# Down projection of a two-layer decoder trunk: the weight sums for the third half-size product, from GpSimd to VectorE

## The chip, the cores and the metric

The kernel runs on one core of one Trainium2 chip. The metric is the device time of one execution in microseconds (us). The kernel before takes 1276.46 us, the median of 3 runs between 1275.83 and 1279.62 us.

## The reference

The reference is a decoder trunk of two layers on 512 tokens of width 1024, in fp32. Layer 0 has sparse attention and a memory cross-attention, layer 1 dilated attention and a memory cross-attention, and each layer ends in the same squared-ReLU MLP. Only the MLP is touched here:

```python
def squared_relu_mlp(h, w_up, w_down):
    return jnp.square(jax.nn.relu(h @ w_up)) @ w_down

x = x + squared_relu_mlp(rmsnorm(x, mlp_norm[layer]), w_up[layer], w_down[layer])
```

`w_up` is 1024 x 4096, `w_down` 4096 x 1024.

## The kernel before

**Precision.** Every fp32 operand of a matrix product is split in a high part (fp32r) and a low part (the rest). `wsplit` does this for weights: ScalarE copies the high part (L237), VectorE subtracts it from the source to get the low part (L239). `split` does it for activations (L282 on ScalarE, L285 on VectorE). `mm3` then issues three matmuls: high by high (L244), and twice high by low (L247), first the one with the low part of the weights, then the one with the low part of the activations.

**The MLP.** The hidden width of 4096 is done in four quarters (the loop over `q` in `mlp`), in each of the two layers, so there are eight quarters in all. A quarter makes eight tiles of 128 hidden columns (the up projection), squares them, and then multiplies them with a 1024 x 1024 block of `w_down`. That product is a Strassen-Winograd scheme: seven products of half size in place of eight. Its operands are sums of blocks. The activation sums are made in `combos` (L1145 and the splits that follow), the weight sums in `addto` (L1131), a loop that adds a loaded block to two tiles of 128 x 512 in place.

**Order of the products in a quarter**, each 24 matmuls for each of two halves `h` of the inner dimension, 48 in all where both halves count:

1. `w11`: block B11 as loaded, into banks of the pool `acc`. Its split is that of a loaded tile `st`. Beside it GpSimd adds B11 to the tiles `U`.
2. `w3`: the pieces `T` (two tiles `x` for each half), which hold B22 - B12 as loaded and summed earlier, into banks of the pool `ps`. After the split, `addto(t, t, b11[h])` adds B11 to the same tiles.
3. `w2`: these new `T`, the third half-size product, into banks of the pool `pt`, against the activation sums `s2` (tiles `act`). After the split, `addto` adds B21 to `T`.
4. `w4`: `T` once more, into the banks `ps` again, which `into` (L1333) has emptied in between.
5. `w1`: the pieces `U`, into new banks `pt`, against `s1`; then `w22` and `w21`, which are blocks as loaded.

So a piece of `T` goes round: split by ScalarE and VectorE, sum, split, sum, split. A sum must wait until both parts of the split before it have been read, and the next split waits for the sum. An instruction of one engine waits for another engine's by a semaphore, and each engine works its own list strictly in order. That order comes from a scheduler that plays the program through; it is fixed when the kernel is built.

**Buffers.** The pool `x` has 8 tiles, `w` 4 split weight tiles, `st` 3 loaded tiles. A tile `st` that holds B11 is free for the next load once the sum that reads it is done.

**First quarter of a layer.** Its VectorE list is further behind TensorE than that of the three others, and the running totals `G` are started by two copies on ScalarE (L1345), where the other quarters add on VectorE (L1337).

Of the kernel before, what the change touches and what calls it, by code (L numbers as in the profile page):

```python
# [12 lines left out]
ALU = mybir.AluOpType  # L13
# [154 lines left out]
class K:  # L168
# [956 lines left out]
            nc.vector.tensor_tensor(out=self.x[m], in0=ps, in1=xo, op=ALU.add)  # L1125


    def addto(self, out, a, b):

        for i, (o, x) in enumerate(zip(out, a)):  # L1130
            self.nc.gpsimd.tensor_tensor(out=o, in0=x, in1=b[:, i * 512 : (i + 1) * 512], op=ALU.add)  # L1131

    def wpieces(self, t):

# [21 lines left out]
    def mlp(self, l):  # L1156


        nc, ins = self.nc, self.ins
        H = S // 2  # L1160
        x = self.x
# [74 lines left out]
        for q in range(4):  # L1236
            a, A12, A4 = [None] * 8, [], []
            B = [ins["w_db"][l, q, i] for i in range(4)]
            U, T = [], []
            for n in range(8):  # L1240
# [32 lines left out]
                if n in (5, 6):  # L1273

                    t = [self.t("x", [P, 512]) for _ in range(2)]
# [16 lines left out]
            b11 = []  # L1292
# [11 lines left out]
            def w3(h):  # L1304

                t = T[2 * h : 2 * h + 2]
                w = self.wpieces(t)
                self.addto(t, t, b11[h])
                return w

            def w2(h):
# [31 lines left out]
            for u in range(2):  # L1343
                if q == 0:
                    nc.scalar.activation(G[u], X[u], AF.Copy)  # L1345
                else:
                    add(G[u], X[u])
            product(Z, blk(0, H), w3)
            into(Z, 1, 1, True)
            Y = two(self.pT)  # L1350
# [463 lines left out]
```

## Time and profile before

| | |
|---|---|
| median of 3 runs | 1276.46 us |
| the profiled execution's own time | 1277.1 us |
| its span, first to last instruction | 1275.3 us |
| mean granted TensorE clock | 0.997 |
| TensorE matmuls busy | 1240.4 us, 97% |
| VectorE busy | 990.8 us, 78% |
| ScalarE busy | 763.3 us, 60% |
| GpSimd busy | 469.4 us, 37% |
| sums on GpSimd (L1131) whose tiles are `x` on both sides | 64, mean 1681 ns |

The row of a timeline holds the start in us, the duration in us (of the whole run of equal instructions, where `xN` is over 1), the engine, the line, the operation with output and inputs, and in brackets how long the engine had stood idle and what released it. In the rows of windows each engine has its busy time and the number of instructions, and PEclk is the granted TensorE clock. A matmul of 512 columns is shown with 0.39 us, but the next one begins about 0.227 us later, so TensorE is filled when starts follow at that distance.

### The profile page before, as it was taken

What the parts mean: (1) busy time and instruction counts of PE and PEld (TensorE: products, weight loads), DVE (VectorE), ACT (ScalarE), POOL (GpSimd) and SP (SyncE); (2) the same over time, 40 slices, a digit from 0 to 9 for tenths busy, and PEclk for the clock granted to TensorE, in tenths of its full rate; (3) what the DMA queues carried; (4) which work ended last, traced back from release to release, by engine and by line L of the source; (5) the groups of instructions that cost most, each with busy time, mean ns of one, the idle gap of its engine ahead of it and who ended that gap; (6) DMA issues with size and microseconds to landing.
All of it is one profiled execution on the core that took longest, in us unless ns stands there. A gap on an engine that the chain in (4) does not pass through costs nothing.

```text
span 1275.3 us, 18580 instructions
## 1 busy us (share of the span) xinstructions
PE 1240.4 (97%) x6445; PEld 1013.5 (79%) x6445; DVE 990.8 (78%) x1745; ACT 763.3 (60%) x1763; POOL 469.4 (37%) x497
## 2 busy tenths in 40 slices
PE   9998999999999999999999999999999999999998
PEld 8776777677787887888888899888688788888886
DVE  6868878864669678687799968887679868779687
ACT  6666767773466464554656567887776455464462
POOL 0666464533165142260342612222435226034241
PEclk9999999999999999999999999999999999999999
DMA  8312311023432525325235332113241532624423
GB/s 312 112 58 69 100 34 59 10 75 106 151 99 77 175 79 171 125 83 185 97 98 179 104 116 64 62 35 96 69 155 67 178 124 79 187 94 139 141 83 116
DMA packets 52718, 139.11 MB, mean 109 GB/s; under 512 B 5680, under 2 KB 14896, under 8 KB 52624
## 3 DMA queue, kind: packets, MB, share of 16 engines
q1 hardware_dynamic: 51568, 135.50, 33.4%
q0 software_dynamic: 480, 1.38, 0.3%
q8 instruction: 51, 0.84, 0.3%
q10 hardware_dynamic: 576, 1.05, 0.2%
q14 instruction: 43, 0.35, 0.1%
HBM read 132.66 MB, written 5.24 MB: 108 GB/s over the span
## 4 chain that ended last, share of the span: by engine, by line
PE 74%; DVE 17%; ACT 4%; issue 2%; DMA 1%; POOL 1%; SPq 0%; POOLq 0%; DVEq 0%; ACTq 0%
PE s_ps L247 23%; PE s_acc L247 12%; PE s_ps L244 11%; DVE s_w L239 6%; PE s_acc L244 6%; PE s_pt L247 5%; PE s_pt L244 3%; DVE s_p L1145 2%; PE s_po L1080 2%; DVE s_qk L285 1%; PE s_acc L845 1%; ACT s_w L237 1%; PE s_pt L1067 1%; PE s_ps L1031 1%; DVE s_pt L1333 1%
## 5 line engine op out<-in xcount | busy, mean ns | idle before, releaser
L247 PE MATMUL s_ps<-s_act,s_w 128*128 128x512 f32 x1184 | 366.0, 390 | 0.0
L239 DVE TENSOR_TENSOR s_w<-s_st,s_w 128x1024 fp32r<-128x1024 f32 (+4 forms) x161 | 191.1, 1189 | 133.5 <-ACT s_w L237 133.2
L247 PEld LDWEIGHTS s_ps<-s_act,s_w 128*128 128x128 f32 x1184 | 221.8, 188 | 45.7 <-DVE s_act L285 0.4
L237 ACT ACTIVATE s_w<-s_st 128x1024 fp32r<-128x1024 f32 (+4 forms) x182 | 165.7, 918 | 131.0 <-PE s_pt L247 35.6
L244 PE MATMUL s_ps<-s_act,s_w 128*128 128x512 f32 x592 | 231.6, 393 | 3.1 <-DVE s_x L817 1.7
L247 PE MATMUL s_acc<-s_w,s_act 128*128 128x512 f32 (+2 forms) x608 | 169.7, 360 | 2.0 <-DVE s_w L239 1.5
L1131 POOL TENSOR_TENSOR s_x<-s_x,s_st 128x512 f32<-128x512 f32 x64 | 106.0, 1681 | 90.8 <-DVE s_w L239 90.8
L244 PEld LDWEIGHTS s_ps<-s_act,s_w 128*128 128x128 f32 x592 | 110.9, 188 | 28.4 <-ACT s_act L282 3.2
L247 PEld LDWEIGHTS s_acc<-s_w,s_act 128*128 128x128 f32 x608 | 108.9, 190 | 13.1 <-DVE s_w L239 1.6
L244 PE MATMUL s_acc<-s_w,s_act 128*128 128x512 f32 (+2 forms) x304 | 111.0, 370 | 1.9 <-ACT s_w L237 1.9
L1131 POOL TENSOR_TENSOR s_x<-s_qki,s_st 128x512 f32<-128x512 f32 x16 | 26.5, 1654 | 214.9 <-DMA s_st<-in_w_db_dram 195.3
L676 POOL TENSOR_SCALAR s_p<-s_p,s_cr 128x256 f32<-128x256 f32 (+3 forms) x128 | 68.0, 545 | 71.6 <-DVE s_cr L1043 33.4
L239 DVE TENSOR_TENSOR s_w<-s_x,s_w 128x512 fp32r<-128x512 f32 x96 | 88.7, 965 | 5.6 <-ACT s_w L237 5.6
L247 PE MATMUL s_pt<-s_w,s_act 128*128 128x512 f32 x288 | 90.0, 399 | 2.6 <-DVE s_w L239 2.6
L285 DVE TENSOR_TENSOR s_qk<-s_p,s_qk 128x256 fp32r<-128x256 f32 (+1 forms) x96 | 83.9, 886 | 2.8 <-ACT s_qk L282 1.8
L237 ACT ACTIVATE s_w<-s_x 128x512 fp32r<-128x512 f32 x96 | 56.8, 624 | 41.1 <-POOL s_x L1131 41.1
L247 PE MATMUL s_ps<-s_w,s_qk 128*128 128x512 f32 x256 | 78.5, 393 | 2.5 <-DVE s_w L239 2.5
L247 PE MATMUL s_acc<-s_w,s_qk 128*128 128x512 f32 x256 | 76.4, 390 | 0.1
L282 ACT ACTIVATE s_qk<-s_p 128x256 fp32r<-128x256 f32 (+1 forms) x96 | 47.0, 489 | 45.1 <-DVE s_p L1259 42.8
L247 PEld LDWEIGHTS s_pt<-s_w,s_act 128*128 128x128 f32 x288 | 54.0, 191 | 16.9 <-DVE s_w L239 6.0
L1253 ACT ACTIVATE s_p<-s_ps 128x512 f32<-128x512 f32 x64 | 37.8, 591 | 46.8 <-PE s_ps L247 44.4
L244 PEld LDWEIGHTS s_acc<-s_w,s_act 128*128 128x128 f32 x304 | 57.5, 190 | 7.3 <-ACT s_w L237 2.0
(336 smaller groups left out, 2735.8 us busy)
## 6 DMA issues: line engine op xcount, KB each, us to landing
s_st<-in_w_db_dram SPq DMA_DIRECT2D x80, 512.0 KB, 3.6
s_st<-in_w_up_dram SPq DMA_DIRECT2D x64, 512.0 KB, 3.9
s_st<-in_w_bq_dram SPq DMA_DIRECT2D x16, 384.0 KB, 3.1
s_st<-in_w_ag_dram SPq DMA_DIRECT2D x11, 512.0 KB, 4.0
s_act<-in_w_c_dram SPq DMA_DIRECT2D x8, 512.0 KB, 5.8
s_st<-in_w_mem_dram SPq DMA_DIRECT2D x8, 512.0 KB, 3.6
s_st<-in_w_ao_dram SPq DMA_DIRECT2D x16, 256.0 KB, 2.7
s_tq<-in_w_db_dram SPq DMA_DIRECT2D x16, 256.0 KB, 3.2
```

The costliest lines, as they stand in the source:

```text
L237: self.high = nc.scalar.activation(w[:, 0], st, AF.Copy)
L239: self.low = e.tensor_tensor(out=w[:, 1], in0=st, in1=w[:, 0], op=ALU.subtract)
L244: mm(ps, lh[0], rh[0], start=start, stop=False, skip_group_check=again)
L247: self.last = mm(ps, lh[i], rh[j], start=False, stop=stop and i != wr, skip_group_check=again)
L282: nc.scalar.activation(dst[:, 0], src, AF.Copy)
L285: nc.vector.tensor_tensor(out=dst[:, 1], in0=src, in1=dst[:, 0], op=ALU.subtract)
L676: self.nc.gpsimd.tensor_scalar(out=p, in0=p, scalar1=c, scalar2=1.0, op0=ALU.mult, op1=ALU.mult)
L845: nc.tensor.matmul(ps, tbf[:, i].rearrange("p g c -> p (g c)"), ws[j][:, i * 256 : (i + 1) * 256], start=j == 0 and i == 0, stop=j == 3 an ...
L1080: nc.tensor.matmul(O[x * 64 : x * 64 + 64, q0 + o : q0 + 256], v[:, j, br, :], st[x][br][:, j, o:256], start=half == 0 and br == 1 and j = ...
L1131: self.nc.gpsimd.tensor_tensor(out=o, in0=x, in1=b[:, i * 512 : (i + 1) * 512], op=ALU.add)
L1145: tt = lambda o, x, y, op: nc.vector.tensor_tensor(out=o, in0=x, in1=y, op=op)
L1253: nc.scalar.activation(u, ps, AF.Relu)
```

## The change

`addto` gets an engine as an argument, with GpSimd as before when none is given. The call in `w3`, which adds B11 to the pieces `T` for the product `w2`, gives VectorE. That is four sums of 128 x 512 for each quarter, 32 in all. The sums in `w11`, in `w2` and after the up projection stay on GpSimd.

```diff
-    def addto(self, out, a, b):
+    def addto(self, out, a, b, e=None):
 
         for i, (o, x) in enumerate(zip(out, a)):
-            self.nc.gpsimd.tensor_tensor(out=o, in0=x, in1=b[:, i * 512 : (i + 1) * 512], op=ALU.add)
+            (e or self.nc.gpsimd).tensor_tensor(out=o, in0=x, in1=b[:, i * 512 : (i + 1) * 512], op=ALU.add)
...
             def w3(h):
 
                 t = T[2 * h : 2 * h + 2]
                 w = self.wpieces(t)
-                self.addto(t, t, b11[h])
+                self.addto(t, t, b11[h], nc.vector)
                 return w
```

The scheduler also puts other instructions in another order. First VectorE in the second quarter of layer 0, from the first sum row of the activations (L1145) on, as it was. `s_x_5177`, `5178`, `5223` and `5224` are the four pieces `T`, `s_w_5361` and `s_w_5382` the two weight tiles of the third product, `s_act_5269` the last activation sum that this product reads.

```order
L1145 TENSOR_TENSOR s_p_1277_5265<-s_p_1266_5213,s_p_1275_5259 128x256
L285 TENSOR_TENSOR s_qk_5262<-s_p_1275_5259,s_qk_5262 128x512
L1145 TENSOR_TENSOR s_p_1277_5265<-s_p_1277_5265,s_p_1266_5213 128x256
L1145 TENSOR_TENSOR s_p_1268_5219<-s_p_1275_5259,s_p_1277_5265 128x256
L1337 TENSOR_TENSOR s_raw_4675<-s_acc_5275,s_raw_4675 128x512
L239 TENSOR_TENSOR s_w_5361<-s_x_5177,s_w_5361 128x512
L285 TENSOR_TENSOR s_act_5269<-s_p_1277_5265,s_act_5269 128x512
L285 TENSOR_TENSOR s_x_5272<-s_p_1268_5219,s_x_5272 128x256
L1337 TENSOR_TENSOR s_raw_4676<-s_acc_5276,s_raw_4676 128x512
L239 TENSOR_TENSOR s_w_5361<-s_x_5178,s_w_5361 128x512
L239 TENSOR_TENSOR s_w_5382<-s_x_5223,s_w_5382 128x512
L239 TENSOR_TENSOR s_w_5382<-s_x_5224,s_w_5382 128x512
```

Now the same list with the change, from the third of the four sums on (the first two stand a little ahead of it, each behind the split of its piece).

```order
L1131 TENSOR_TENSOR s_x_5223<-s_x_5223,s_st_5298 128x512
L285 TENSOR_TENSOR s_qk_5262<-s_p_1275_5259,s_qk_5262 128x512
L239 TENSOR_TENSOR s_w_5361<-s_x_5177,s_w_5361 128x512
L1131 TENSOR_TENSOR s_x_5224<-s_x_5224,s_st_5298 128x512
L239 TENSOR_TENSOR s_w_5361<-s_x_5178,s_w_5361 128x512
L1145 TENSOR_TENSOR s_p_1277_5265<-s_p_1277_5265,s_p_1266_5213 128x256
L1337 TENSOR_TENSOR s_raw_4675<-s_acc_5275,s_raw_4675 128x512
L1337 TENSOR_TENSOR s_raw_4676<-s_acc_5276,s_raw_4676 128x512
L239 TENSOR_TENSOR s_w_5382<-s_x_5223,s_w_5382 128x512
L239 TENSOR_TENSOR s_w_5382<-s_x_5224,s_w_5382 128x512
L1145 TENSOR_TENSOR s_p_1268_5219<-s_p_1275_5259,s_p_1277_5265 128x256
L285 TENSOR_TENSOR s_act_5269<-s_p_1277_5265,s_act_5269 128x512
```

The sums stand between the other work, the splits of the third product's weights have moved up, and the low part of the last activation sum (L285 into `s_act_5269`) has moved behind all of them.

VectorE in the first quarter of layer 0 with the change, from the fourth sum to the same activation sum (here `s_act_4627`, and the weight tiles are 4721 and 4742). Before, that L285 stood right behind the first split of 4721.

```order
L1131 TENSOR_TENSOR s_x_4582<-s_x_4582,s_st_4656 128x512
L239 TENSOR_TENSOR s_w_4721<-s_x_4536,s_w_4721 128x512
L1145 TENSOR_TENSOR s_p_1179_4623<-s_p_1179_4623,s_p_1168_4571 128x256
L239 TENSOR_TENSOR s_w_4742<-s_x_4581,s_w_4742 128x512
L239 TENSOR_TENSOR s_w_4742<-s_x_4582,s_w_4742 128x512
L1145 TENSOR_TENSOR s_p_1170_4577<-s_p_1177_4617,s_p_1179_4623 128x256
L285 TENSOR_TENSOR s_act_4627<-s_p_1179_4623,s_act_4627 128x512
```

There are no L1337 rows in it, and the activation sum is again last.

TensorE in the second quarter of layer 0, second half of the third product, as it was:

```order
L244 MATMUL s_pt_5359<-s_w_5382,s_act_5171 128x512
L247 MATMUL s_pt_5359<-s_w_5382,s_act_5171 128x512 x2
L244 MATMUL s_pt_5359<-s_w_5382,s_act_5269 128x512
L247 MATMUL s_pt_5359<-s_w_5382,s_act_5269 128x512 x2
L244 MATMUL s_pt_5360<-s_w_5382,s_act_5171 128x512
L247 MATMUL s_pt_5360<-s_w_5382,s_act_5171 128x512 x2
L244 MATMUL s_pt_5360<-s_w_5382,s_act_5269 128x512
L247 MATMUL s_pt_5360<-s_w_5382,s_act_5269 128x512 x2
```

And with the change:

```order
L244 MATMUL s_pt_5359<-s_w_5382,s_act_5171 128x512
L244 MATMUL s_pt_5360<-s_w_5382,s_act_5171 128x512
L247 MATMUL s_pt_5359<-s_w_5382,s_act_5171 128x512 x2
L244 MATMUL s_pt_5359<-s_w_5382,s_act_5269 128x512
L247 MATMUL s_pt_5360<-s_w_5382,s_act_5171 128x512
L247 MATMUL s_pt_5359<-s_w_5382,s_act_5269 128x512
L247 MATMUL s_pt_5360<-s_w_5382,s_act_5171 128x512
L244 MATMUL s_pt_5360<-s_w_5382,s_act_5269 128x512
L247 MATMUL s_pt_5360<-s_w_5382,s_act_5269 128x512
L247 MATMUL s_pt_5359<-s_w_5382,s_act_5269 128x512
L247 MATMUL s_pt_5360<-s_w_5382,s_act_5269 128x512
```

The two banks are mixed, so that the first matmul that needs the low part of `s_act_5269` (the last row but one) is the eleventh here and was the sixth. In the first quarter of each layer this half of the product keeps its old order. All the same moves stand in the other quarters of both layers; GpSimd's list only loses the 32 sums.

## The prediction
> **What bounds the kernel now.** I read the page first.
>
> ```profile
> span 1275.3 us, 18580 instructions
> ...
> PE 1240.4 (97%) x6445; PEld 1013.5 (79%) x6445; DVE 990.8 (78%) x1745; ACT 763.3 (60%) x1763; POOL 469.4 (37%) x497
> ...
> L1131 POOL TENSOR_TENSOR s_x<-s_x,s_st 128x512 f32<-128x512 f32 x64 | 106.0, 1681 | 90.8 <-DVE s_w L239 90.8
> ```
>
> TensorE is the bound nearly everywhere, so the change is worth only the gaps in TensorE that hang on these sums. To find them I took stretches of TensorE's timeline that hold 48 matmuls of 512 columns each. The first below is the second product, w3, in the second quarter of layer 0; the eight others run from the start of the third product, w2, to the start of w1 (so w2 and w4) in the eight quarters, in order.
>
> ```profile
> 474.44:485.32 10.88, 10.88 (x50) 9.01 (x48) 9.95 (x11) 6.00 (x12) 8.11 (x5) 1.00 0.31 96
> 400.91:414.60 13.69, 12.03 (x50) 8.70 (x48) 13.69 (x19) 8.62 (x16) 6.74 (x4) 1.00 0.46 144
> 485.32:497.10 11.78, 11.40 (x50) 8.85 (x48) 11.78 (x18) 5.56 (x9) 5.07 (x3) 1.00 0.42 124
> 567.82:579.50 11.68, 11.26 (x50) 8.85 (x48) 11.68 (x18) 5.45 (x9) 5.08 (x3) 1.00 0.41 119
> 650.22:661.88 11.66, 11.28 (x50) 8.85 (x48) 11.66 (x17) 5.45 (x9) 5.08 (x3) 1.00 0.28 90
> 992.06:1006.89 14.83, 13.33 (x49) 9.90 (x48) 14.83 (x20) 8.66 (x16) 6.72 (x4) 0.88 0.45 146
> 1077.61:1089.26 11.65, 11.27 (x49) 8.86 (x48) 11.65 (x17) 5.45 (x9) 5.08 (x3) 1.00 0.40 120
> 1159.98:1171.72 11.74, 11.40 (x49) 8.85 (x48) 11.74 (x17) 5.55 (x9) 5.07 (x3) 1.00 0.42 129
> 1242.44:1254.37 11.93, 11.54 (x49) 8.86 (x48) 11.93 (x18) 5.67 (x9) 5.06 (x3) 1.00 0.29 89
> ```
>
> 48 matmuls without a gap take 10.88 us, 0.227 each. The eight stretches lose 2.81, 0.90, 0.80, 0.78, 3.95, 0.77, 0.86 and 1.05, together 11.92 us: 5.16 in the six later quarters and 6.76 in the two first ones. More than 11.92 us is not to be had here, and the third number of each row (VectorE or DVE, busy from end to end in the eight) says who is late. The timeline of TensorE in the first quarter:
>
> ```profile
> 400.91 0.39 PE L244 MATMUL s_pt<-s_w,s_act 128*128 128x512 f32 x1
> 401.59 0.73 PE L247 MATMUL s_pt<-s_w,s_act 128*128 128x512 f32 x2 [0.29 <-DVE s_w L239]
> ...
> 404.22 1.20 PE L247 MATMUL s_pt<-s_w,s_act 128*128 128x512 f32 x4 [0.99 <-DVE s_w L239]
> ...
> 492.41 0.73 PE L247 MATMUL s_ps<-s_w,s_qk 128*128 128x512 f32 x2 [0.38 <-DVE s_w L239]
> ```
>
> TensorE waits for the low parts of the third product's weights, and in the second quarter (492.41) for those of the fourth. The first matmul pair after a wait takes 0.73 for 0.62: a restart costs 0.11.
>
> Why VectorE is late, in its timeline and GpSimd's (POOL), first quarter and then second:
>
> ```profile
> 392.32 4.69 DVE L239 TENSOR_TENSOR s_w<-s_x,s_w 128x512 fp32r<-128x512 f32 x4
> 413.40 0.68 DVE L239 TENSOR_TENSOR s_w<-s_qki,s_w 128x512 fp32r<-128x512 f32 x1
> 414.00 0.68 DVE L239 TENSOR_TENSOR s_w<-s_tq,s_w 128x512 fp32r<-128x512 f32 x1
> ...
> 473.61 1.29 DVE L239 TENSOR_TENSOR s_w<-s_x,s_w 128x512 fp32r<-128x512 f32 x2
> 475.79 2.51 DVE L239 TENSOR_TENSOR s_w<-s_x,s_w 128x512 fp32r<-128x512 f32 x2 [0.89 <-ACT s_w L237]
> 478.22 1.51 DVE L1145 TENSOR_TENSOR s_p<-s_p,s_p 128x256 f32<-128x256 f32 x1
> 479.65 1.77 DVE L285 TENSOR_TENSOR s_qk<-s_p,s_qk 128x512 fp32r<-128x512 f32 x1
> 481.34 0.87 DVE L1145 TENSOR_TENSOR s_p<-s_p,s_p 128x256 f32<-128x256 f32 x2
> 482.13 0.68 DVE L1337 TENSOR_TENSOR s_raw<-s_acc,s_raw 128x512 f32<-128x512 f32 x1
> 488.87 0.74 DVE L1333 SCALAR_TENSOR_TENSOR s_pt<-s_ps,n,s_pt 128x512 f32<-128x512 f32 x1
> ```
>
> ```profile
> 393.08 6.50 POOL L1131 TENSOR_TENSOR s_x<-s_x,s_st 128x512 f32<-128x512 f32 x4 [7.42 <-DVE s_w L239]
> ...
> 474.37 6.50 POOL L1131 TENSOR_TENSOR s_x<-s_x,s_st 128x512 f32<-128x512 f32 x4 [7.42 <-DVE s_w L239]
> ...
> 486.73 5.07 POOL L1131 TENSOR_TENSOR s_x<-s_x,s_st 128x512 f32<-128x512 f32 x3 [1.56 <-DVE s_w L239]
> ```
>
> Undisturbed, VectorE's instructions with two inputs in SBUF follow each other at 0.60 us for 512 elements (413.40, 414.00) and at about 0.40 for 256. While GpSimd makes its four sums, 474.37 to 480.87, they take 1.77 and 1.51: VectorE gets one in for each sum of 5.07 / 3 = 1.69 us, done 0.55 after the sum's end (479.65 + 1.77 = 481.42 against 480.87; for 256 I take half). I call this the lock. An instruction with an input in PSUM (L1333 at 488.87, amid three sums) keeps its 0.74. So a GpSimd sum costs VectorE 1.69 - 0.60 = 1.1 us of its time.
>
> **The change, part by part.** *Removed:* the four sums of 6.50 us on GpSimd, and the lock on VectorE during them. *Added:* four instructions on VectorE. The trace has no fp32 sum of these shapes there; the nearest row, L239 (two inputs in SBUF, 512), gives 0.60 each, 2.4 us a quarter. That is also the lower bound, as no row of 512 is followed sooner; the upper is 1.69, if each still met a GpSimd sum. I take 0.60, since only the type of the output differs from L239's, and GpSimd rests where they stand (idle 7.42 before its row at 474.37). On GpSimd only the sums in w2 are left near; they now begin earlier and lock VectorE there.
>
> *Later quarters (six).* I lay the new list beside the second quarter's times. The two splits of piece 1 and 2 start at 473.61 and 474.21, sum 1 at 474.81; the next split keeps 475.79, where ScalarE releases it; sum 2 at 476.39, split 476.99, L1145 477.59, sum 3 477.99, L285 478.59, first split of the third product 479.19 to 479.87, sum 4 to 480.47. ScalarE has the high parts in time: it is busy for half of these stretches. At 479.87 the first w2 sum may start on GpSimd; from here one VectorE instruction with two SBUF inputs fits per sum. Sums end near 481.55, 483.85, 486.2, 487.9; the second split ends at 482.1, L1145 and the two L1337 (one input in PSUM) fit behind it, the third split ends at 484.4 and the fourth at 485.0, L1145 at 486.5, and the last activation sum, L285 into `s_act_5269`, at 487.9 + 0.55 = 488.45. TensorE starts w2 at 485.32; weights are there 2.5 us ahead, and it needs that sum's low part as the eleventh matmul of the second half: 485.32 + (24 + 10 - 12) x 0.227 = 490.3. It is 1.85 us early. The splits for w4 then run undisturbed from 488.4 (0.60 each, with two L1333 between), the fourth done at 492.4, needed after 493.8. So no wait is left: 5.16 us gained. What covers the added 2.4 us is the 1.85 us and the removed lock; without cover they would come back as a wait at L285.
>
> *First quarters (two).* Here VectorE begins the same list at 392.32 with TensorE's w2 at 400.91, 8.59 ahead in place of 485.32 - 473.61 = 11.71. By the same steps: sums at 393.52, 394.72, 396.32 and 398.12, splits of the third product done at 398.2 and 400.5, so the waits of now at 401.59 and 404.22 go. But the w2 sums lock VectorE from 398.25: third split at 402.75, fourth 403.35, L1145 404.8, and L285 only when the fourth sum has ended, 406.2 + 0.55 = 406.75. TensorE, in the old order there, needs it as the sixth matmul of the second half: 400.91 + 17 x 0.227 = 404.77. **A new wait of 2.0, with the restart 2.1 us**, takes the place of 2.81 and 3.95: gains 0.7 and 1.85. Bounds of this new wait: 0.7 (one lock less, L285 done at 405.4) to 3.8 (one lock of 1.69 more).
>
> The 3.95 holds a clock gap:
>
> ```profile
> 991.00:995.40 4.40, 2.91 (x11) 1.46 (x9) 4.37 (x8) 3.70 (x8) 1.67 (x1) 1.00 0.39 121
> 995.40:999.00 3.60, 3.59 (x9) 2.80 (x10) 3.60 (x4) 1.10 (x3) 3.56 (x3) 0.53 0.22 38
> ```
>
> After a stretch with 11 matmuls, about 2.5 us of work, in 4.40 us, the granted clock was 0.53 for 3.6 us and only 9 more went in, where 3.6 / 0.227 = 15.9 would have: about 1.6 us lost. The first quarter of layer 0 has the same waits and no such gap, so it comes in some places by chance. I count it gone: the new wait is in one piece of 2.0 us, with full work on both sides. If it comes, 1.6 us of the gain in that quarter is lost.
>
> The Trainium skill, "TensorE: Matmul & The Clock Gate", Part 1, has TensorE fall to half clock after at least one idle window of about 3.4 us, free-running. By that rule a wait of 2.0 us would never cost the clock and the sum stays as it is. This case's trace differs: the clock fell although 11 matmuls ran in the 4.40 us ahead, so I leave the gap a chance.
>
> *Other.* VectorE's total grows by 32 x 0.60 = 19 us but loses about 32 x 1.1 = 35 us of lock. Loads into tiles `st` that wait for the sums are issued a little earlier, which nothing waits for. The end of layer 0 has a few rows in another order; I cost it at nothing, since TensorE is filled there; it may be 0.5 us either way.
>
> **Sum:** 5.16 + 0.7 + 1.85 = 7.7 us off the profiled execution's 1277.1: **1269.4 us**. The median of the runs lies 0.64 below that execution, which may be part of the clock gap; I leave the number.
>
> **Rivals.** *The first quarters lose their wait too.* If L285 goes ahead of the fourth w2 sum there, the new waits are 0.7 each: 5.16 + 2.1 + 3.25 = 10.5 off, 1266.6; and without any wait 11.92 off, 1265.2. Against it: in the rows above GpSimd gets its next sum in after every single instruction of VectorE.
>
> *The wait moves in the later quarters.* If VectorE comes to L285 two locks later there than laid out (3.4 us, where 1.85 are in hand; one lock would still fit), say because the two L1337 wait for the first product and stand in the way, these quarters wait 1.55 + 0.11 = 1.66 where they now wait 0.86 on average. With two of the six so, 1272.7; with four, 1276.0; with all, 1279.4. That is within 0.3% of the median (3.8 us, about what a measurement of this kernel can tell from no change). For it: VectorE is busy from end to end in these stretches.
>
> *Slower: VectorE becomes the bound.* If the added sums cost their upper bound, 1.69, L285 in the later quarters is 4 x 1.09 = 4.4 us later, so it waits 2.5, as long as a first quarter, and the clock gap follows in two of five: 6 x (2.6 + 0.6 - 0.86) = 14, and the first quarters wait 4.4 longer, 2 x 4.4 = 8.8, less 2.55: near 1297. It decides from about 2.7 us more on VectorE's list than laid out, for all eight quarters. Against it: the 0.60 of L239 in the rows above.
>
> *The change does nothing* can't be: the order has the sums on VectorE, and no wait for GpSimd is left ahead of w2.
>
> **Numbers.** Forecast 0.62; first quarters free too 0.12; wait moved 0.17; slower 0.09. Faster by over 0.3% (below 1272.6) is the first two, less 0.04 for a forecast with clock gaps and a longer wait in both first quarters: 0.70. Within 0.3%: 0.21. Slower: 0.09. The range reaches from the end of the second case, 1265.2, to four of the six quarters of the third, 1276.0; what is left out is the slower case and the upper part of the third, about 0.16.
>
> **What would show it.** L1131 as a VectorE group of 32 near 680 ns busy, and GpSimd's group of 64 down to 32. The eight stretches from w2 to w1: six at 10.9 to 11.1, two at about 13.0, with the wait named L285 `s_act`. L239 on pieces `x` (965 ns mean now) nearer 800. Wrong: waits for L285 or L237 in the later quarters, VectorE sums over 1 us, or half clock in more than one place.

## The result and the profile after

The changed kernel takes 1268.03 us, the median of 6 runs between 1265.80 and 1270.76 us; the kernel before, beside it, 1277.7 us (6 runs, 1275.83 to 1279.62). The ratio is 0.9924, with a 95% interval from 0.9908 to 0.9941, so 9.7 us are gained. The forecast was 1269.4 us, 7.7 under the profiled execution of before. The profiled execution took 1267.84 us, 9.3 less than that of before.

The page of the changed kernel, its head and the row of the GpSimd sums, and from the groups by line the row of the sums that moved:

```profile
span 1266.0 us, 18595 instructions
...
PE 1234.1 (97%) x6445; PEld 1013.9 (80%) x6445; DVE 966.9 (76%) x1777; ACT 763.6 (60%) x1763; POOL 438.9 (35%) x465
...
L1131 POOL TENSOR_TENSOR s_x<-s_x,s_st 128x512 f32<-128x512 f32 x32 | 75.8, 2401 | 102.9 <-DVE s_w L239 102.9
```

```profile
L1131 DVE TENSOR_TENSOR s_x<-s_x,s_st 128x512 f32<-128x512 f32 x32 | 21.9, 684 | 0.0
```

VectorE has 32 instructions more and is busy for 24 us less. GpSimd has half the sums, but those left last 2401 ns in the mean, where the 64 of before lasted 1681: some of them now wait for VectorE. In a later quarter these are the first two of the four sums in w2 (2.62 us at 479.04 and 3.98 at 481.62), in the first quarter of layer 0 the first alone (4.75, shown below).

The same eight stretches, from the start of w2 to the start of w1 (length, then busy time and count of each engine, then PEclk):

```profile
401.61:413.74 12.13, 11.18 (x49) 8.93 (x48) 10.29 (x16) 5.93 (x10) 6.91 (x4) 1.00 0.46 154
484.46:495.34 10.88, 10.88 (x49) 9.01 (x48) 9.20 (x14) 5.36 (x9) 4.10 (x3) 1.00 0.55 172
566.06:576.94 10.88, 10.88 (x49) 9.01 (x48) 9.19 (x14) 5.37 (x9) 4.09 (x3) 1.00 0.58 173
647.66:658.54 10.88, 10.88 (x49) 9.01 (x48) 9.20 (x14) 5.36 (x9) 4.09 (x3) 1.00 0.32 97
989.08:1000.69 11.61, 11.19 (x49) 8.93 (x48) 9.77 (x14) 5.93 (x10) 6.38 (x4) 1.00 0.46 144
1071.41:1082.29 10.88, 10.88 (x49) 9.01 (x48) 9.19 (x14) 5.36 (x9) 4.09 (x3) 1.00 0.54 171
1153.01:1163.89 10.88, 10.88 (x49) 9.01 (x48) 9.19 (x14) 5.36 (x9) 4.09 (x3) 1.00 0.59 172
1234.61:1245.49 10.88, 10.88 (x49) 9.01 (x48) 9.19 (x14) 5.36 (x9) 4.09 (x3) 1.00 0.34 98
```

Six stretches are at the 10.88 us of 48 matmuls without a gap. The two first quarters lose 1.25 and 0.73. Of 11.92 us, 1.98 are left: 9.94 gained in the stretches, against 9.3 for the whole execution. VectorE is no longer busy from end to end in any of them. A word on counting: a product takes 24 matmuls, 12 for each of its two halves, and not 24 for each half, so the 48 of a stretch are w2 and w4; the stretch without a gap that stands first in the prediction holds w11 and w3 in the same way, and not w3 alone.

The first quarter of layer 0, VectorE, with the sums in w2 on GpSimd beside it and the one wait of TensorE:

```profile
399.57 0.68 DVE L239 TENSOR_TENSOR s_w<-s_x,s_w 128x512 fp32r<-128x512 f32 x1
400.17 0.41 DVE L1145 TENSOR_TENSOR s_p<-s_p,s_p 128x256 f32<-128x256 f32 x1
400.50 1.28 DVE L239 TENSOR_TENSOR s_w<-s_x,s_w 128x512 fp32r<-128x512 f32 x2
401.71 0.41 DVE L1145 TENSOR_TENSOR s_p<-s_p,s_p 128x256 f32<-128x256 f32 x1
402.04 0.68 DVE L285 TENSOR_TENSOR s_act<-s_p,s_act 128x512 fp32r<-128x512 f32 x1
404.57 1.10 DVE L239 TENSOR_TENSOR s_w<-s_x,s_w 128x512 fp32r<-128x512 f32 x1 [1.84 <-ACT s_w L237]
405.59 0.74 DVE L1333 SCALAR_TENSOR_TENSOR s_pt<-s_ps,n,s_pt 128x512 f32<-128x512 f32 x1
406.25 1.12 DVE L239 TENSOR_TENSOR s_w<-s_x,s_w 128x512 fp32r<-128x512 f32 x1
407.30 1.51 DVE L285 TENSOR_TENSOR s_x<-s_p,s_x 128x256 fp32r<-128x256 f32 x1
408.73 0.74 DVE L1333 SCALAR_TENSOR_TENSOR s_pt<-s_ps,n,s_pt 128x512 f32<-128x512 f32 x1
```

```profile
399.12 4.75 POOL L1131 TENSOR_TENSOR s_x<-s_x,s_st 128x512 f32<-128x512 f32 x1 [12.57 <-DVE s_w L239]
...
479.04 2.62 POOL L1131 TENSOR_TENSOR s_x<-s_x,s_st 128x512 f32<-128x512 f32 x1 [13.04 <-DVE s_w L239]
```

```profile
409.52 0.50 PE L244 MATMUL s_ps<-s_w,s_qk 128*128 128x512 f32 x1 [0.95 <-DVE s_pt L1333]
```

The first sum of w2 begins at 399.12 and takes 4.75 us. In that time VectorE runs six instructions with two inputs in SBUF, 0.60 us apart for 512 columns and 0.33 for 256, as if GpSimd did not exist. L285 into `s_act`, for which a wait was forecast, is done at 402.72 and nobody waits for it. The sum ends at 403.87, 1.15 after VectorE's last row. What is late is the next step. The first split for w4 waits for that sum (404.57, by way of ScalarE's L237). The three sums that follow hold VectorE up (1.10, 1.12, 1.51), so the second L1333, which empties the second bank of w3, ends at 409.47, and the first matmul of w4 into that bank waits.

### The profile page after: what moved, and what is told of

It reads as the page before. It is cut to its first block, busy times and chain, and to the rows that moved or that the text cites. A ratio compares the mean times of both kernels' runs of the same rounds, so it can differ in the third digit from the quotient of the medians.

```text
span 1266.0 us, 18595 instructions
## 1 busy us (share of the span) xinstructions
PE 1234.1 (97%) x6445; PEld 1013.9 (80%) x6445; DVE 966.9 (76%) x1777; ACT 763.6 (60%) x1763; POOL 438.9 (35%) x465
## 4 chain that ended last, share of the span: by engine, by line
PE 79%; DVE 12%; ACT 4%; issue 2%; POOL 2%; DMA 2%; SPq 0%; POOLq 0%; DVEq 0%; ACTq 0%
PE s_ps L247 23%; PE s_acc L247 13%; PE s_ps L244 12%; PE s_pt L247 7%; PE s_acc L244 6%; PE s_pt L244 4%; DVE s_w L239 2%; PE s_po L1080 1%; ACT s_w L237 1%; PE s_acc L845 1%; PE s_pt L1067 1%; PE s_ps L1541 1%; DVE s_p L1145 1%; PE s_ps L1031 1%; DVE s_w L263 1%
## 5 line engine op out<-in xcount | busy, mean ns | idle before, releaser
L239 DVE TENSOR_TENSOR s_w<-s_st,s_w 128x1024 fp32r<-128x1024 f32 (+4 forms) x161 | 191.8, 1195 | 140.2 <-ACT s_w L237 140.0
L237 ACT ACTIVATE s_w<-s_st 128x1024 fp32r<-128x1024 f32 (+4 forms) x182 | 165.7, 918 | 140.8 <-PE s_pt L247 40.7
L1131 POOL TENSOR_TENSOR s_x<-s_x,s_st 128x512 f32<-128x512 f32 x32 | 75.8, 2401 | 102.9 <-DVE s_w L239 102.9
L1131 POOL TENSOR_TENSOR s_x<-s_qki,s_st 128x512 f32<-128x512 f32 x16 | 26.2, 1638 | 220.4 <-DMA s_st<-in_w_db_dram 200.7
L237 ACT ACTIVATE s_w<-s_x 128x512 fp32r<-128x512 f32 x96 | 57.3, 625 | 54.9 <-POOL s_x L1131 36.5
L247 PE MATMUL s_pt<-s_w,s_act 128*128 128x512 f32 x288 | 86.8, 390 | 0.0
L239 DVE TENSOR_TENSOR s_w<-s_x,s_w 128x512 fp32r<-128x512 f32 x96 | 67.8, 726 | 12.5 <-ACT s_w L237 12.2
L285 DVE TENSOR_TENSOR s_qk<-s_p,s_qk 128x256 fp32r<-128x256 f32 (+1 forms) x96 | 75.1, 795 | 2.8 <-ACT s_qk L282 1.9
```

What stands on the lines that cost most here:

```text
L237: self.high = nc.scalar.activation(w[:, 0], st, AF.Copy)
L239: self.low = e.tensor_tensor(out=w[:, 1], in0=st, in1=w[:, 0], op=ALU.subtract)
L247: self.last = mm(ps, lh[i], rh[j], start=False, stop=stop and i != wr, skip_group_check=again)
L285: nc.vector.tensor_tensor(out=dst[:, 1], in0=src, in1=dst[:, 0], op=ALU.subtract)
L1131: (e or self.nc.gpsimd).tensor_tensor(out=o, in0=x, in1=b[:, i * 512 : (i + 1) * 512], op=ALU.add)
```

## The experiments

The theory is that of the prediction: a GpSimd sum holds VectorE up by 1.1 us, VectorE is the late engine, and each quarter stands by itself. Rivals are the handover (split, sum and split on two engines, with a semaphore between), and the new order of the lists. The sums in w2 add a question: why does the first of them hold VectorE up no longer? All times are medians, each with its ratio to the kernel before on the same chip.

### One half of the quarters at a time

First quarters only, and then the six others only:

```diff
-                self.addto(t, t, b11[h], nc.vector)
+                self.addto(t, t, b11[h], nc.vector if q == 0 else None)
```

> The four sums are on VectorE in the first quarter of each layer only; the six later quarters are as before. Theory (the lock: each GpSimd sum holds VectorE up by 1.1 us, and VectorE is the late engine in each quarter by itself): the quarters gain apart from each other, so the two first ones bring what they bring in the whole change, 2.81 + 3.95 - 1.25 - 0.73 = 4.8 us, of which 1.6 is the clock gap: 3.2 to 4.8 us under the kernel before, about 1272 to 1274, with the six later stretches still at 11.65 to 11.95 us. Rival (the new order of the lists brings the gain, or the quarters hang on one another): less than 2 us, or the later quarters change too.

```diff
-                self.addto(t, t, b11[h], nc.vector)
+                self.addto(t, t, b11[h], nc.vector if q else None)
```

> The other half: sums on VectorE in the six later quarters only, the first quarter of each layer as before. Theory (the lock, each quarter by itself): the six stretches come to 10.88 us and bring 5.16 us, so about 1272 us, 5.2 under the kernel before; the first quarters stay at 13.7 and at 13.2 to 14.8 us. Together with the kernel that does only the first quarters the gains add up to that of the whole change (9.7 by the medians). Rival (quarters hang on one another): the gains don't add up by more than 2 us.

Measured: 1273.99 us (ratio 0.9979, 0.9968 to 0.9991) for the first quarters, 1273.49 us (0.9966, 0.9952 to 0.9981) for the later ones; before 1277.11. Two stretches of the first kernel, two of the second, and for the second and the kernel before the stretch between the layers:

```profile
401.25:413.17 11.92, 11.22 (x49) 8.93 (x48) 10.07 (x15) 5.95 (x10) 6.67 (x4) 1.00 0.44 148
483.89:495.55 11.66, 11.27 (x49) 8.86 (x48) 11.66 (x17) 5.45 (x9) 5.08 (x3) 1.00 0.39 127
```

```profile
484.43:495.31 10.88, 10.88 (x49) 9.01 (x48) 9.19 (x14) 5.36 (x9) 4.09 (x3) 1.00 0.56 170
992.38:1006.03 13.65, 12.08 (x49) 8.70 (x48) 13.65 (x19) 8.55 (x16) 6.74 (x4) 1.00 0.43 141
...
660.00:983.00 323.00, 315.96 (x1898) 271.24 (x1897) 255.54 (x544) 231.19 (x653) 102.76 (x126) 0.98 0.31 96
```

```profile
660.00:983.00 323.00, 315.82 (x1914) 270.40 (x1914) 259.58 (x551) 232.49 (x655) 102.70 (x126) 1.00 0.31 96
```

Each quarter keeps its own gain: a changed first quarter has 11.92 with 11.66 behind it (the other unchanged ones lie between 11.65 and 12.15), a changed later one 10.88. In the stretches the quarters stand by themselves, as the theory has it. The medians do not add up: 3.1 and 3.6 make 6.7, not 9.7. By my own bound of 2 us that speaks for the rival, but the missing 3 us do not lie in the stretches. From the start of w2 in the last quarter of layer 0 to that in the first quarter of layer 1 the two profiled executions take 343.94 (992.91 - 648.97) and 344.75 us (992.38 - 647.63), that of before 341.84 and that of the changed kernel 341.42. All engines' lists there are those of before in the first kernel, and those of the changed kernel in the second, up to the last 8 us ahead of the first quarter. So it is not the order. The granted clock between the layers was 0.99 in the first kernel and 0.98 in the second, and 1.00 before. The intervals allow a sum of 9.7 too: 1.1 to 4.1 and 2.4 to 6.1 us.

The second kernel also gives the clock gap its size: its first quarter of layer 1 has the waits of before, and takes 13.65 at a clock of 1.00, where the profiled execution of before took 14.83 at 0.88. The lists of all engines around that quarter are the same in both kernels. The gap was 1.2 us, and it came in one execution and not in the other.

### The old sums put back beside the new ones

```diff
+        idle = self.sb.tile([P, 448], F32, name=f"idle{l}", tag="rb", bufs=1)
...
                 self.addto(t, t, b11[h], nc.vector)
+                for i in range(2):
+                    c = slice(i * 512, i * 512 + 448)
+                    nc.gpsimd.tensor_tensor(out=idle, in0=b11[h][:, c], in1=w[:, 1, c].bitcast(F32), op=ALU.add)
```

> The sums stay on VectorE, and GpSimd makes again four sums of 448 columns at the place of the old ones, of the same loaded block and the low part of the split, into a tile that nobody reads; nothing waits for them. Theory (the lock): VectorE is held up again, 4 x 0.9 us in each quarter, with 2.4 us of sums more on its list than before; the stretches come back to 12 us or more, the time to that of the kernel before or above (1277 to 1290), and the VectorE rows beside the idle sums are near 1.7 us. Rival (what was slow was the handover, split to GpSimd and back to the split, and the sum's own time on GpSimd): nothing waits for the idle sums, so the time stays within 1.5 us of the changed kernel, 1267 to 1269.5. A third way: GpSimd doesn't get its turn while VectorE is busy, as in the changed kernel's first sums of w2 (4750 ns): then the idle sums last over 2.5 us each, and the time stays near 1268 because the lock isn't taken.

Measured: 1298.37 us, 1.0166 (1.0146 to 1.0186). Two of its stretches, a GpSimd row, and VectorE beside it:

```profile
400.25:419.06 18.81, 14.36 (x50) 10.49 (x48) 18.21 (x23) 7.01 (x12) 7.71 (x5) 0.82 0.44 137
489.78:502.91 13.13, 11.44 (x49) 8.85 (x48) 13.13 (x19) 6.51 (x11) 4.89 (x4) 1.00 0.48 149
```

```profile
486.89 1.67 POOL L1131 TENSOR_TENSOR s_x<-s_x,s_st 128x512 f32<-128x512 f32 x1 [2.77 <-DVE s_w L239]
```

```profile
480.86 1.65 DVE L239 TENSOR_TENSOR s_w<-s_x,s_w 128x512 fp32r<-128x512 f32 x1
...
486.73 0.68 DVE L1131 TENSOR_TENSOR s_x<-s_x,s_st 128x512 f32<-128x512 f32 x1
487.33 1.78 DVE L239 TENSOR_TENSOR s_w<-s_x,s_w 128x512 fp32r<-128x512 f32 x1
```

No instruction waits for an idle sum, and still 30 us are lost against the changed kernel: VectorE's rows beside them go from 0.68 to 1.65 us, and VectorE is busy for 13.13 of 13.13. The idle sums also take time in GpSimd's own list: in the first quarter the fourth (402.10 to 403.69) stands ahead of the second sum of w2. But what TensorE waits for in w2 there are rows of VectorE, L239 (0.89 and 1.07 us) and L285 (2.49). The handover is not needed to explain the loss, and neither is the order, which is that of the changed kernel but for a few rows. Whether the sums would gain as much on VectorE with the old order around them, no run shows. The time is over the range that I gave (1277 to 1290): a clock fall lies in the stretch shown at 0.82 and in five more of the eight (0.82 to 0.89). In this kernel the w2 sums, 2.8 us behind an idle sum, hold VectorE up again (1.67 us, and 1.78 for the L239 that follows), with the same row L1131 in flight as in the changed kernel, where that sum takes 2.62 and VectorE runs on.

### A small sum ahead of w2

Since the sums in w2 behaved in one way after 12.6 us of rest or more and in another after 2.8, this kernel takes the idle sums at 16 columns in place of 448. No other engine's order changes.

```diff
-        idle = self.sb.tile([P, 448], F32, name=f"idle{l}", tag="rb", bufs=1)
+        idle = self.sb.tile([P, 16], F32, name=f"idle{l}", tag="rb", bufs=1)
...
-                    c = slice(i * 512, i * 512 + 448)
+                    c = slice(i * 512, i * 512 + 16)
```

> The changed kernel with four sums of only 16 columns on GpSimd at the place of the old ones, into a tile that nobody reads; no other engine's order changes. Before, GpSimd had rested 7.4 us or less ahead of its sums, and took its turn after each VectorE instruction; with the change it has rested 12.6 us or more ahead of the w2 sums, and VectorE runs on while the sum lasts 2616 to 4750 ns. With idle sums of 448 columns, 2.8 us ahead, it took its turn again at the same place (1672 ns). Theory (the rest decides who goes first): with the small sums GpSimd rests under 8 us, the w2 sums last about 1.7 us each and hold VectorE up; the first quarters then wait for L285 as predicted, near 13.0 us each in place of 12.13 and 11.61, the later ones stay near 10.88: 1269 to 1271. Rival (the rest doesn't decide, the size of the sum ahead or the phase does): the first w2 sum still lasts over 2.6 us, and the time stays within 1 us of the changed kernel, 1267 to 1269.

Measured: 1268.98 us, 0.9936 (0.9916 to 0.9955). The first quarters, the first w2 sum, VectorE beside the sums, and TensorE's wait:

```profile
403.84:416.62 12.78, 11.21 (x49) 8.93 (x48) 12.78 (x18) 6.61 (x11) 4.35 (x3) 1.00 0.47 151
991.70:1004.19 12.49, 11.19 (x50) 8.93 (x48) 12.49 (x17) 6.47 (x11) 4.08 (x3) 1.00 0.41 147
```

```profile
401.38 1.68 POOL L1131 TENSOR_TENSOR s_x<-s_x,s_st 128x512 f32<-128x512 f32 x1 [1.83 <-DVE s_w L239]
```

```profile
401.83 1.78 DVE L239 TENSOR_TENSOR s_w<-s_x,s_w 128x512 fp32r<-128x512 f32 x1
...
407.61 1.75 DVE L285 TENSOR_TENSOR s_act<-s_p,s_act 128x512 fp32r<-128x512 f32 x1
```

```profile
409.42 0.50 PE L247 MATMUL s_pt<-s_w,s_act 128*128 128x512 f32 x1 [1.56 <-DVE s_act L285]
```

A few columns ahead are enough to bring back the case that the forecast worked out: GpSimd takes its turn, L285 into `s_act` comes last, and TensorE waits for it, 1.90 and 1.61 us over 10.88 where 2.1 was forecast for each. The six later quarters keep 10.88 (487.34 to 498.22 in the second). The total lies 1 us over the changed kernel, where the ranges of theory and rival meet, and the two intervals overlap, so it is the rows that speak here and not the total. Against the kernel before this one, only the length of the idle sums and a few rows of the order differ, and 29 of the 30 us are gone: an idle sum costs by its length, and not by its place in the lists. So the forecast's working of the first quarters was right for the case in which GpSimd takes turns, and the changed kernel is not that case.

### What decides the turn: two programs of their own

Neither computes anything of the reference. Chains of VectorE rows with two inputs in SBUF, back to back, and one GpSimd sum released by a chosen row (`at`, counted from 0 in the code and from 1 in the text); `keep` holds the order as written, and before each chain ScalarE makes `delay` copies, in which GpSimd rests:

```diff
+            for kinds, at, delay in VARIANTS:
...
+                for i, k in enumerate(kinds):
...
+                    if k == "L":
+                        v = nc.vector.tensor_tensor(out=lo[:, c(i % 8)], in0=xi, in1=h, op=ALU.subtract)
...
+                    if i == at:
+                        keep(nc.gpsimd.tensor_tensor(out=x[at], in0=x[at], in1=st[0][:, 0:512], op=ALU.add))
```

> A program of its own, which computes nothing of the reference: chains of 8 or 12 VectorE instructions with two inputs in SBUF back to back, with one GpSimd sum of 128 x 512 that is released by the second (or sixth) of them; five chains (only L239's form; one with an in-place sum in flight; one with a split of 1024 columns and then one of 256 columns; one with an input in PSUM as the fifth; one of twelve), each after seven lengths of rest of GpSimd, from about 6 to 40 us, twice. Theory (the rest decides): after a rest under some bound between 8 and 12.5 us the sum lasts near 1.67 us and the next VectorE row lasts near 1.78; after longer rests the sum lasts until the chain ends or comes to the row with an input in PSUM, 4 to 8 us, and no VectorE row is over 0.75. Rival (the kind of the rows decides): the length of the sum goes by the chain and not by the rest.

Two neighbours in the program's GpSimd timeline, the chain of twelve and then that of eight:

```profile
47.87 4.65 POOL L70 TENSOR_TENSOR x<-x,st 128x512 f32<-128x512 f32 x1 [8.15 <-DVE lo L55]
58.33 1.58 POOL L70 TENSOR_TENSOR x<-x,st 128x512 f32<-128x512 f32 x1 [5.81 <-DVE lo L55]
```

The rest theory fell. At every rest, 3.3 to 45 us, the chains of eight had their sum next, near 1577 ns (2110 with a split of 1024 columns in flight); and at every rest, 8 to 48 us, the chain of twelve made it wait for its end, 4650 ns, fourteen times in fourteen. The kind of the rows decided nothing either: an in-place sum in flight gave the same 1577. What differed is that the sum was released by the second row in one and by the sixth in the other.

> The same kind of program, which computes nothing of the reference, since in the one before neither the rest of GpSimd nor the kind of the rows decided: there the sum released by the second row of a chain always went next (1577 ns), and the one released by the sixth of twelve always waited for the end (4652 ns). Here chains of fourteen rows of 512 columns, with the sum released by row 2, 3, 4, 5, 6, 7, 8 and 9; of 256 columns, released by row 2, 4, 6, 8, 10, 12; and of 512 with a row that reads PSUM as the sixth, released by row 5 to 9. Theory (the number of VectorE rows back to back since a pause or since GpSimd's last turn decides): with 512 columns the sum goes next up to row 4 or 5 (near 1577 to 1680 ns) and from then on lasts to the end of the chain, 0.6 us less for each row later (from row 6: 14 - 7 = 7 rows left, 5.9 us); with 256 columns the same rows decide. Second way (the time back to back decides, about 3.2 to 3.8 us): with 256 columns, 0.34 to 0.4 us a row, the change comes at row 8 to 10. The row that reads PSUM lets a waiting sum in (2.0 to 2.7 us for release by row 5); if it also starts the count anew, the sums released by row 7 to 9 go next. Third way (the phase of the release in VectorE's row decides, 228 ns against 162 after its start): the sum's length jumps with the phase and not steadily with the row.

The GpSimd timeline of this program: 512 columns, released by row 5 and row 6; 256 columns, by row 4 and row 6; and with a row that reads PSUM as the sixth, by row 5, 6 and 7.

```profile
59.90 1.59 POOL L64 TENSOR_TENSOR x<-x,st 128x512 f32<-128x512 f32 x1 [12.51 <-DVE lo L57]
74.01 5.80 POOL L64 TENSOR_TENSOR x<-x,st 128x512 f32<-128x512 f32 x1 [12.52 <-DVE lo L57]
...
137.36 1.31 POOL L64 TENSOR_TENSOR x<-x,st 128x512 f32<-128x512 f32 x1 [8.92 <-DVE y L59]
147.59 3.66 POOL L64 TENSOR_TENSOR x<-x,st 128x512 f32<-128x512 f32 x1 [8.92 <-DVE y L59]
...
188.79 1.26 POOL L64 TENSOR_TENSOR x<-x,st 128x512 f32<-128x512 f32 x1 [7.34 <-DVE lo L57]
202.58 1.57 POOL L64 TENSOR_TENSOR x<-x,st 128x512 f32<-128x512 f32 x1 [12.53 <-DVE y L61]
216.61 5.25 POOL L64 TENSOR_TENSOR x<-x,st 128x512 f32<-128x512 f32 x1 [12.45 <-DVE lo L57]
```

A sum is released at the end of its row and so meets the row behind it in flight. Released by rows 2, 3, 4 and 5, the sum went next (1.58 to 1.64 us); by row 6, 7, 8 and 9 it waited for the end of the chain of fourteen, 5.80, 5.20, 4.60 and 4.0 us, one row of 0.60 less each. The last turn is had with the sixth row in flight, none with the seventh. With 256 columns the change lies between the same rows (4 and 6), at 1.6 to 2.2 us in place of 3.2 to 3.8: rows count, not time. The phase doesn't decide: 162 and 228 ns after the start of the row in flight stand on both sides. A row that reads PSUM lets a waiting sum in (1.26), but it neither counts nor starts the count anew: the sum released by the PSUM row itself, with the sixth row of two SBUF inputs in flight, goes next (1.57), and the sum released by the row behind it, with the seventh in flight, waits to the end (5.25).

This fits the kernels. Before, nearly every sum held VectorE up and so, by this reading, began the count again. The kernel with the small sums bears that out: its w2 sum at 401.38 also comes with the twelfth row since VectorE's last pause in flight, but with the fourth since the last small sum, and it goes next (1.68). With the four sums gone from GpSimd, VectorE, counted from its last pause, has its eighth row back to back in flight when the first w2 sum comes in a later quarter, and its twelfth in a first one, and none of these eight sums goes next; in a later quarter it gets in at L1337, which reads PSUM (2.62 us). Why it is six was not tried, and neither were rows of other types or other lengths than 512 and 256.

### The sums in w2 on VectorE as well

```diff
-                self.addto(t, t, self.wdma(B[2][h]))
+                self.addto(t, t, self.wdma(B[2][h]), nc.vector)
```

> On top of the change, the four sums that make the next weights (B21 added in w2) go to VectorE as well. Theory (the lock): what is left, 1.25 and 0.73 us in the two first quarters, is the wait for L239, L285 and L1333, which the w2 sums on GpSimd lock; they go, and the six others stay at 10.88: 2.0 us under the changed kernel, near 1266. Rival (VectorE's own load): 2.4 us more in each stretch make VectorE late for w4 or w1 in some quarters: 1268 to 1280, with waits for L239 or L1333 in the later quarters.

Measured: 1274.16 us, 0.998 (0.9964 to 0.9996): 6 us over the changed kernel. From w2 to the next w2, first and second quarter, then VectorE and TensorE behind w2:

```profile
401.28:482.88 81.60, 81.60 (x362) 67.58 (x360) 64.04 (x92) 42.64 (x68) 13.27 (x8) 1.00 0.42 133
482.88:565.38 82.50, 81.90 (x361) 67.51 (x360) 62.73 (x89) 42.10 (x66) 12.99 (x8) 1.00 0.39 128
```

```profile
496.68 1.41 DVE L1333 SCALAR_TENSOR_TENSOR s_pt<-s_ps,r,s_pt 128x512 f32<-128x512 f32 x2 [3.12 <-PE s_ps L247]
498.00 2.35 DVE L239 TENSOR_TENSOR s_w<-s_st,s_w 128x1024 fp32r<-128x1024 f32 x2
```

```profile
500.41 0.72 PE L247 MATMUL s_acc<-s_w,s_qk 128*128 128x512 f32 x2 [0.60 <-DVE s_w L239]
```

The first quarters are free of waits (81.60, where the changed kernel takes 82.85), so the mechanism named for them is right. The later quarters lose 0.9 each, which the changed kernel does not. It is the rival's place (L239 and L1333), but by the rows not its reason: VectorE is not overloaded, it stands idle for 3.12 us. Its list has L1333 ahead of the splits of the loaded weights, L1333 waits for w4 on TensorE, whose last matmuls the scheduler now mixes with those of w1, and the splits queue behind it. That is read from the lists; no run changed this order alone. Four such quarters, and 3.9 us at the end of layer 1, where the same wait runs into a clock fall (0.77 in 1256 to 1262), outweigh the 2.0 gained; the part between the layers took 3.5 us longer in this execution.

### Only where it was missing

```diff
-                self.addto(t, t, self.wdma(B[2][h]))
+                self.addto(t, t, self.wdma(B[2][h]), nc.vector if q == 0 else None)
```

> On top of the change, the sums in w2 go to VectorE in the first quarter of each layer only (eight sums), where 1.25 and 0.73 us were left; the six other quarters stay as in the changed kernel. Theory: with all of w2 on VectorE the first quarters came to 10.88 us and the loss came back behind them, 0.86 us in each later quarter at the split of the loaded weights (wait for L239 at 500.41 in that kernel); with the first quarters alone nothing comes back: 2.0 us under the changed kernel, near 1266, and under both kernels. Rival (what comes back is not bound to the later quarters, but to these sums on VectorE wherever they are): the first quarters lose as much behind w1 as they gain, 1267.5 to 1270.

Measured: 1265.88 us, 0.9909 (0.9887 to 0.993), 6 runs. To tell it from the changed kernel, both were run once more on one chip.

> The changed kernel as it is, once more, beside the version with the first quarters' w2 sums on VectorE, on one chip: 9.2 to 9.9 us under the kernel before.

> The version with the first quarters' w2 sums on VectorE, once more beside the changed kernel. By the stretches (1.25 and 0.73 us left in the changed kernel, nothing here) 2.0 us under the changed kernel and 11.5 to 12 under the kernel before; the rival, that the end of the first quarters gives part of it back or that the half clock between the layers comes oftener, gives less than 1 us.

Measured: the changed kernel 1267.75 us, 0.9924 (0.9909 to 0.9939); this version 1267.34 us, 0.9921 (0.9906 to 0.9935). A first quarter of the version in this second run, and a part of layer 0 far ahead of the change:

```profile
402.50:413.38 10.88, 10.88 (x49) 9.01 (x48) 10.88 (x20) 5.62 (x10) 0.00 (x0) 1.00 0.54 175
...
118.00:130.00 12.00, 10.64 (x44) 8.02 (x43) 6.88 (x15) 9.36 (x24) 5.83 (x6) 0.78 0.48 149
```

All eight stretches are at 10.88 in both profiled executions of it: the 2.0 us are gained where they were forecast. But the time holds only 0.4 of them the second time. That execution reached the first w2 2.0 us later than the changed kernel beside it (402.50 against 400.50), after a granted clock of 0.78 in 118 to 130, where that one had 0.86; whether this makes all of the 2.0 us is not shown. Over both measurements of each kernel the medians are 1266.6 and 1267.8, 12 runs each: better by 1.2 us as they stand, and not told apart by the intervals.

## Why the prediction came out as it did

**What bounds the kernel, and where the 11.92 us lie: right.** 9.94 of them went, and the rest of the execution moved by 0.7 us the other way.

**The cost of a sum on VectorE, 0.60: right.** The rows are 684 ns long, and start 0.60 apart.

**The lock as the cause: right for the sums that were moved.** Idle sums at their place bring the loss back, and more, with nothing that waits for them: 36.4 us are lost in the eight stretches with 448 columns, clock falls included, and 3.5 with 16.

**Six later quarters gain all 5.16: right.** All six are at 10.88. In the changed kernel this does not test the layout of the forecast, since GpSimd did not take its turns there: L285 into `s_act` was done at 483.84, ahead of w2 (484.46). With the small sums GpSimd takes turns as the forecast assumed, and L285 is done 2.74 us after the start of w2 (490.08 against 487.34), where 3.13 was laid out, and nothing waits.

**The first quarters, new wait of 2.1 each: wrong.** The step that failed is "from here one VectorE instruction with two SBUF inputs fits per sum". I had taken a rule from rows in which every sum of GpSimd came within a few rows of the last one. The change itself ended that: it lets VectorE run on, and beyond the sixth row back to back GpSimd gets no turn. L285 into `s_act` came at 402.72 and not at 406.75. The wait that is left is another one, at L1333 and w4, and smaller, 1.25 and 0.73. The first rival, that L285 goes ahead of the fourth w2 sum there, is the nearest to what happened: L285 went ahead of the end of all four. Its 0.7 for each quarter (1266.6 in all) was the price of a shorter wait at L285, though, and that wait went altogether. That the forecast lies only 1.4 us off is in part luck: 4.2 us of wait that did not come were made up in part by 1.98 of another that no step had.

**The clock gap: right that it goes, wrong in size.** It was 1.2 us and not 1.6. Without it the first quarters' gains are 1.56 and 2.04 (13.65 - 11.61), where 0.7 and 0.25 were forecast.

**The sum.** 5.16 + 0.7 + 1.85 = 7.7 forecast; 5.16 + 1.56 + 3.22 = 9.94 in the stretches, 9.3 between the profiled executions, 9.7 between the medians. The 2.2 us that the forecast lacks are the two waits of 2.1 at L285 that did not come, less the 1.98 at L1333 that did.

**Slower, VectorE as the bound: did not come.** With the sums of w2 on VectorE too, a loss of 0.9 in each later quarter does come, but, as its rows read, by the order of its list and not by its load.

## What to carry over

When two engines hold each other up, take the rows of both and see who gets the next turn, and ask of a change whether it alters the pattern from which the rule was read: a sum of 1.69 us became one of 4.75 because the sums ahead of it were gone. Idle work at the old place, read by nobody, separates what an instruction costs by being there from what its result costs by being late. A gain of 2 us that the stretches show can drown in clock falls elsewhere: compare the stretch as well as the total.

## What the runs showed of the hardware

GpSimd's turn against VectorE goes by the number of VectorE rows with two SBUF inputs back to back: up to the sixth in flight it goes next, from the seventh it waits until the chain ends or a row reads PSUM (1.59 against 5.80 us for one row of difference; fp32 rows of 512 columns; with 256 the change lies between the fifth and the seventh). A pause of VectorE starts the count again, and so does a sum that goes in between two such rows (1.68 for the twelfth row behind a pause that is the fourth behind a small sum); a row that reads PSUM does not (5.25). The Trainium skill, "SBUF — State Buffer", the section on the two separate sides, has VectorE, with two inputs in SBUF, and GpSimd share a pair of ports that goes to whoever starts first, for the whole instruction, while the other blocks. The single rows agree (1.78 for an L239 behind a sum, 0.68 alone). By that rule alone a waiting sum would come in at the next end of a row, and the 4.75 us do not agree with it unless a chain counts as one holder.

The granted clock falls in places that change from one execution to the next of the same lists: the first quarter of layer 1 with the waits of before had 0.88 in one execution and 1.00 in another, a difference of 1.2 us in that stretch.
